# Squares summed on TensorE ahead of two feed-forward stages, and spare matmuls in three places

## The chip, the cores and the metric

The kernel runs on one core of one Trainium2 chip, in one launch. Times are device microseconds of that core. PE is TensorE (matrix products, its results go to PSUM), DVE is VectorE, ACT is ScalarE, POOL is GpSimd and SP is SyncE, which issues most of the transfers. "Granted clock" is the share of full speed at which the profile shows TensorE to run. The metric is the time of one execution. Three runs of the kernel before took 1934.97, 1938.0 and 1938.1 us, median 1938.0.

## The reference

The program computes two layers of a trunk over 512 latent and 256 context tokens of width 1024, all in fp32. Both layers follow the same plan. Layer 0 mixes by differential attention beside a gated DeltaNet, layer 1 by neighbourhood attention on a 64-wide grid; only the latent tokens leave layer 1.

```python
def rms_norm(x, gain):
    xf = x.astype(f32)
    y = xf * lax.rsqrt(jnp.mean(xf * xf, axis=-1, keepdims=True) + EPS)
    return (y * gain.astype(f32)).astype(x.dtype)

def swiglu(h, w_in, w_out):
    gt, up = jnp.split(h @ w_in, 2, axis=-1)
    return (jax.nn.silu(gt) * up) @ w_out
...
        h = rms_norm(x, norm_mix[l]) * (1.0 + sc_m) + sh_m
...
        x = x + g_m * o                      # o: the mixer's output
        hf = rms_norm(x, norm_ffn[l]) * (1.0 + sc_f) + sh_f
        x = x + g_f * swiglu(hf, ffn_w_in[l], ffn_w_out[l])
```

The vectors `sh`, `sc`, `g` come from the conditioning vector by a matrix `ada_w`. The change touches how three of the four `rms_norm` are scheduled, and how two of them sum their squares.

## The kernel before

**Layout.** The activations lie feature-major: `x[k]`, k = 0 to 7, is a tile of 128 features by 768 tokens, the first 256 of them context (`CTX`), the rest latent (`LAT`). Where tokens are treated in pieces, `SEGS` names three segments of 256 tokens: the context and two latent halves. A sum over the features of a token is thus a sum over the eight tiles and over the 128 partitions.

**Products.** Each fp32 product is made of three matmuls of split operands: a high part in the type fp32r and a low part that holds the rest. `mm3` (its matmul is L180) issues high x high, high x low and low x high into one PSUM tile. Weights are split by ACT (a copy, L166) and DVE (a subtraction, L167) in `wsplit`; in the first FFN by `split` (L1519, L1520). Activations are split by the same pair.

**Order.** A framework places the instructions: the program is written as a sequence, and a list scheduler with its own timeline of costs sets the order in which each engine's queue issues them. Each queue is in order afterwards. Buffers come from pools with a tag and a number of buffers; a tile waits for the one that had its buffer before. The PSUM pool `gs` has three tags, A and B with three banks and C with two. So an instruction that is added in one place can move others elsewhere.

**The stages in time.** The first norm is at about 5 to 64 us, the layer-0 mixer up to 680, its output product with the norm ahead of the first FFN (n0f) to about 750, the first FFN and the mixing norm of layer 1 (n1m) to about 1260, the layer-1 mixer to 1550, its output product with the norm ahead of the second FFN (n1f) to 1580, then the second FFN to the end.

**The first norm** (L460 to L560) squares on ACT, adds on DVE (L474), sums over partitions by six matmuls with a vector of ones (L489), and makes the reciprocal root. Then `modulate(j)` makes the scales and shifts of two of the eight tiles: 32 small matmuls (`acc`, L509) from a matrix `aw` that two transfers bring, a copy to a row (DVE, L514), a transpose on TensorE into the PSUM tile `tp` (L516), and the scaling itself, whose results are split into `hhi` (ACT, L534) and `hlo` (DVE, L535). `dense(j, ...)` multiplies these two tiles with the first weights into six PSUM tiles `vp` (L548). The two functions alternate, j = 0 to 3.

**The other norms** are objects of `Norm`. `acc(k, i)` squares tile k of segment i on ACT (L322) and adds the square to `ssq` (L324): on POOL for k below a number, on DVE from it on. `finish(i)` sums over partitions by one matmul for each 128 tokens with the vector of ones as moving operand (L335, PSUM tile `sp`, tag C), takes mean plus epsilon on ACT (`ms`, L337), makes the reciprocal root by a seed and three Newton steps (`rsqrt`, L194 to L206: one operation on DVE, the rest on POOL), and broadcasts it over the partitions with an identity matrix as moving operand (L341, `rb`, tag C). Then eight scalings by DVE (`nt`, L344) read `rb` from PSUM, and `put` shifts and splits them. For the first FFN, `NormS.put` writes them with ACT into `hf` (L383), and `half(0)` and `half(1)` form sums and differences and split them (`split`: ACT L399, DVE L400) into the `v` tiles and others, because this FFN uses the Strassen-Winograd scheme; its products `f` are 128 x 384. The second FFN takes `hhi` and `hlo` (L356, L357) straight, its `f` are 128 x 256 and 128 x 512.

The table `NORMS` gives for each norm the number k from which DVE adds, the engine of the root (G is POOL), and tiles whose split POOL helps with:

```python
NORMS = dict(n0f=(5, 'G', (7,)), n1m=(5, 'G', (7,)), n1f=(4, 'G', ()))
```

**The two places ahead of the FFNs.** For each segment, the loop at L1424 to L1442 makes the eight output tiles of the layer-0 mixer (`o`, six matmuls each for the last two heads, tags A and B), adds them to `x[c]` on DVE (L1435), calls `acc`, and after the eighth `finish`, and from the second segment on `half`. POOL also adds the first weights of the FFN there (`prep`, L1477 to L1480, `ws`), 1.3 us for 512 columns. In layer 1, `oproj` (L1829) does the same for two latent halves (L1866 to L1869), with three matmuls for a tile at the end.

## Time and profile before

| | us |
|---|---|
| median of the three runs | 1938.0 |
| the profiled execution, its own time | 1938.09 |
| its span in the trace | 1936.3 |
| TensorE busy | 1794.5 |
| DVE busy | 1257.4 |
| ACT busy | 805.2 |
| POOL busy | 380.5 |
| TensorE's wait for the reciprocal roots of POOL, all norms | 26.8 |
| mean granted clock | 0.967 |

The slices in the page cut the span into 40 equal parts of 48.4 us; a digit is the busy share of an engine in tenths, and in the row `PEclk` the granted clock. Rows of the table of stretches give the borders in us from the start of the span, the length, the busy time of PE, PEld (loading of weights), DVE, ACT and POOL with their instructions, the granted clock, and the share and rate of the transfers. Rows of a timeline give the start, the duration, the engine, the line, the operation and, in brackets, for how long the engine stood still before it and what ended that. A group's row gives count, busy time, mean duration in ns and the idle time before it.

### The profile page before, as it was taken

Reading aid. Unit: us, or ns where it says so; the run is one execution under the profiler, and the core shown is the slowest. Engines: PE = TensorE matmul, PEld = TensorE weight load, DVE = VectorE, ACT = ScalarE, POOL = GpSimd, SP = SyncE. Lnnn points to the kernel's source line nnn. Section 1 sums busy time; section 2 is a strip of 40 time slices with the busy share of each in tenths; the row PEclk is TensorE's granted clock in tenths of the full one; section 3 lists DMA queues with packets and bytes.
Section 4 is the critical chain, followed back from the end, with each engine's and each line's share of the span. In section 5 each row is a group of like instructions: output and inputs, shape, how many; then the busy total and the mean of one; then the engine's idle time right before and its main releaser. Section 6 shows DMA issues by size and latency. Waiting matters only on the chain.

```text
span 1936.3 us, 30405 instructions
## 1 busy us (share of the span) xinstructions
PE 1794.5 (93%) x11343; PEld 1623.0 (84%) x11343; DVE 1257.4 (65%) x2839; ACT 805.2 (42%) x1773; POOL 380.5 (20%) x436
## 2 busy tenths in 40 slices
PE   4979999788988958999999999899999989999999
PEld 3867889677877857999999999899999778888887
DVE  6566688676767569988877878746666663433333
ACT  3434454446465355232323323455555342222221
POOL 2132214441201052141231322401010020000000
PEclk8989999899999979999999999899999989999999
DMA  7466645656344622424344334212111212323232
GB/s 300 147 192 206 208 128 151 187 158 196 115 122 152 210 83 66 131 98 124 109 138 138 122 122 133 91 45 77 56 62 45 88 45 87 111 78 119 87 105 92
DMA packets 114436, 238.43 MB, mean 123 GB/s; under 512 B 11920, under 2 KB 51088, under 8 KB 113136
## 3 DMA queue, kind: packets, MB, share of 16 engines
q1 hardware_dynamic: 101760, 208.32, 33.8%
q0 software_dynamic: 4064, 14.38, 2.6%
q10 hardware_dynamic: 8464, 13.79, 2.0%
q8 instruction: 90, 1.47, 0.3%
q14 instruction: 58, 0.48, 0.1%
HBM read 203.44 MB, written 32.99 MB: 122 GB/s over the span
## 4 chain that ended last, share of the span: by engine, by line
PE 72%; DVE 6%; DMA 5%; ACT 3%; POOL 2%; issue 2%; SPq 0%; POOLq 0%; ACTq 0%; DVEq 0%
PE f L180 43%; PE d L180 16%; PE o L180 3%; DMA qkd<-ar 1%; PE sc L1779 1%; PE o L1804 1%; PE m L954 1%; PE S L1250 1%; PE t L1278 1%; DMA st<-in_ada_w_dram 1%; PE m L1793 1%; DVE e L1264 0%; PE m L1052 0%; PE m L1750 0%; PE m L1066 0%
## 5 line engine op out<-in xcount | busy, mean ns | idle before, releaser
L166 ACT ACTIVATE whi<-st 128x1024 fp32r<-128x1024 f32 (+6 forms) x191 | 169.6, 889 | 402.7 <-PE f L180 234.3
L167 DVE TENSOR_TENSOR wlo<-st,whi 128x1024 fp32r<-128x1024 f32 (+6 forms) x191 | 195.9, 1027 | 147.7 <-ACT whi L166 145.6
L180 PE MATMUL d<-whi,hhi 128*128 128x256 f32 (+1 forms) x800 | 235.3, 296 | 18.0 <-ACT ar L211 13.6
L180 PE MATMUL d<-wlo,hhi 128*128 128x256 f32 (+1 forms) x800 | 233.2, 292 | 1.3 <-DVE wlo L167 1.3
L180 PE MATMUL d<-whi,hlo 128*128 128x256 f32 (+1 forms) x800 | 232.7, 292 | 0.0
L180 PE MATMUL f<-hlo,whi 128*128 128x512 f32 (+2 forms) x632 | 229.2, 363 | 2.6 <-DVE hlo L400 2.3
L180 PE MATMUL f<-hhi,whi 128*128 128x512 f32 (+2 forms) x632 | 228.5, 363 | 2.6 <-DVE ev L1549 1.3
L180 PE MATMUL f<-hhi,wlo 128*128 128x512 f32 (+2 forms) x632 | 228.2, 362 | 0.3 <-DVE wlo L1520 0.3
L180 PEld LDWEIGHTS d<-whi,hhi 128*128 128x128 f32 x800 | 157.2, 197 | 24.1 <-ACT ar L211 14.9
L180 PEld LDWEIGHTS d<-wlo,hhi 128*128 128x128 f32 x800 | 157.5, 197 | 2.5 <-DVE wlo L167 1.7
L180 PEld LDWEIGHTS d<-whi,hlo 128*128 128x128 f32 x800 | 157.0, 197 | 1.0
L180 PE MATMUL f<-mid,whi 128*128 128x512 f32 (+1 forms) x624 | 151.5, 337 | 0.0
L180 PE MATMUL f<-v,whi 128*128 128x384 f32 x528 | 138.4, 341 | 3.5 <-ACT v L399 2.2
L180 PEld LDWEIGHTS f<-hlo,whi 128*128 128x128 f32 x632 | 119.5, 189 | 16.6 <-DVE hlo L400 2.8
L180 PEld LDWEIGHTS f<-hhi,whi 128*128 128x128 f32 x632 | 119.3, 189 | 16.4 <-ACT hf L383 1.6
L180 PEld LDWEIGHTS f<-hhi,wlo 128*128 128x128 f32 x632 | 119.5, 189 | 13.6 <-DVE wlo L1520 0.5
L180 PEld LDWEIGHTS f<-mid,whi 128*128 128x128 f32 x624 | 106.9, 189 | 12.8
L1477 POOL TENSOR_TENSOR ws<-st 128x512 f32<-128x512 f32 x22 | 33.3, 1511 | 406.0 <-DMA st<-in_wfi_dram 289.9
L180 PE MATMUL d<-hhi,whi 128*128 128x512 f32 (+1 forms) x304 | 107.7, 354 | 2.8 <-ACT cin L211 1.4
L180 PE MATMUL d<-hhi,wlo 128*128 128x512 f32 (+1 forms) x304 | 105.5, 348 | 0.0
L180 PE MATMUL d<-hlo,whi 128*128 128x512 f32 (+1 forms) x304 | 105.4, 347 | 0.0
L180 PE MATMUL f<-mid,wlo 128*128 128x256 f32 (+1 forms) x312 | 102.5, 336 | 0.0
(410 smaller groups left out, 4348.5 us busy)
## 6 DMA issues: line engine op xcount, KB each, us to landing
st<-in_wfi_dram SPq DMA_DIRECT2D x88, 512.0 KB, 3.3
ast<-in_ada_t_dram SPq DMA_DIRECT2D x96, 256.0 KB, 2.9
st<-in_ada_w_dram SPq DMA_DIRECT2D x32, 512.0 KB, 4.0
aw<-in_ada_dram SPq DMA_DIRECT2D x8, 1024.0 KB, 12.5
st<-in_wfo_dram SPq DMA_DIRECT2D x32, 256.0 KB, 2.9
st<-in_w1kv_dram SPq DMA_DIRECT2D x16, 512.0 KB, 3.2
aqT<-qkd SPq DMA_DIRECT2D x48, 128.0 KB, 3.1
st<-in_wfo_dram SPq DMA_DIRECT2D x16, 384.0 KB, 3.0
```

What stands on the lines that cost most here:

```text
L166: S.activation(out=hi, in_=st, func=AF.Copy)
L167: last_lo[:] = [V.tensor_tensor(out=lo, in0=st, in1=hi.bitcast(F32), op=ALU.subtract).ins]
L180: r = T.matmul(out=ps, lhsT=p, rhs=q, start=(c == 0), stop=(c == n - 1))
L954: T.matmul(out=ps[:, i, :], lhsT=lhs[:, c, :], rhs=rhs[:, c, :], start=True, stop=True)
L1250: T.matmul(out=ps[:, o:o + w], lhsT=u.q[:, part, :], rhs=kst[:, m, sl], start=(i == 0), stop=(i == 1))
L1278: T.matmul(out=ov, lhsT=PT[:, i, :], rhs=vt[:, u.kts[i], :], start=(i == 0), stop=(i == u.nk - 1))
L1477: G.tensor_tensor(out=sa[:, 0:512], in0=a21, in1=a22, op=ALU.add)
L1779: T.matmul(out=o, lhsT=lq[:, q], rhs=kv(lk), start=(i == 0), stop=(i == 2))
L1793: T.transpose(out=tp[:, 128 * i:128 * i + 128], in_=E[:, qi, 128 * b:128 * b + 128], identity=ident)
L1804: T.matmul(out=o, lhsT=lv[:, v, :], rhs=p, start=(n == 0 and i == 0), stop=(n == 5 and i == 2))
```

## The change

Three things are changed.

1. For n0f and n1f the squares are no longer added on POOL and DVE. Each square tile goes to TensorE at once: for each 128 tokens one matmul with the square as stationary operand and the vector of ones as moving operand, accumulating over k in one PSUM tile of tag C. n0f has 48 such matmuls where it had 6, n1f 32 where it had 4. The buffers for squares are four instead of two, for n1m too, which otherwise stays as it was.
2. A new function `warm` issues a chain of matmuls of an identity matrix with itself, 128 x 128, into a PSUM tile that nothing reads. It is called with 22 behind the last `o` of n0f, with 16 behind the last `o` of n1f, and with 30 behind the transpose of the first `modulate`, there in the bank of `tp`, which is widened to a whole bank.
3. `mm3`, `oproj` and `modulate` return their last matmul, after which the chain is ordered.

```diff
--- before.py
+++ after.py
@@ -32,7 +32,8 @@
 RS_SEED = -1.8352575e-20
 
 ORDER = "vp0 out1 Ad0 Bd1 vp1 Bd2 Bd3 Ad1 Ad2 G2 G0 Ad3 G1 G3".split()
-NORMS = dict(n0f=(5, 'G', (7,)), n1m=(5, 'G', (7,)), n1f=(4, 'G', ()))
+WARM = (22, 16, 30)
+NORMS = dict(n0f=(None, 'G', (7,)), n1m=(5, 'G', (7,)), n1f=(None, 'G', ()))
 FILL = dict(out1=2, Ad0=1, vp1=2, Ad2=1, G2=3, Ad3=1, G1=3)
 
 CONST_W = {}
@@ -185,6 +186,14 @@
                         tc.add_manual_dep(g.ins, r.ins.name, dep, reason="pace")
                         nops.append(g.ins)
                     c += 1
+            return r.ins
+
+        def warm(pool, tag, pred, n):
+            t = pool.tile([128, 512], F32, name="warm", tag=tag)
+            for _ in range(n):
+                d = T.matmul(out=t[:, 0:128], lhsT=ident, rhs=ident, start=True, stop=True).ins
+                tc.add_manual_dep(d, pred.name, after, reason="warm")
+                pred = d
 
         def rsqrt(pool, v, n, tag="rs", N=None):
             N = N or V
@@ -316,9 +325,21 @@
                 s, sl = self.segs[i]
                 n = sl.stop - sl.start
                 first = self.ssq[i] is None
+                if self.on_v is None:
+                    if first:
+                        self.ssq[i] = self.ps.tile([128, 512], F32, name="sp", tag="C")
+                    sq = self.tile("sq", 256, 4)
+                    S.activation(out=sq, in_=self.x[k][:, sl], func=AF.Square)
+                    m = n // 128
+                    for j in range(m):
+                        self.last = T.matmul(
+                            out=self.ssq[i][:, j:j + 1], lhsT=sq[:, 128 * j:128 * j + 128], rhs=ones,
+                            start=(k == 0 and j == 0), stop=(k == KT - 1 and j == m - 1),
+                        ).ins
+                    return
                 if first:
                     self.ssq[i] = self.tile(f"ssq{i}", n)
-                sq = self.ssq[i] if first else self.tile("sq", 256, 2)
+                sq = self.ssq[i] if first else self.tile("sq", 256, 4)
                 S.activation(out=sq, in_=self.x[k][:, sl], func=AF.Square)
                 if not first:
                     (V if k >= self.on_v else G).tensor_tensor(out=self.ssq[i], in0=self.ssq[i], in1=sq, op=ALU.add)
@@ -330,8 +351,8 @@
                 if self.h is None:
                     self.h = new_h()
                 hi, lo = self.h
-                sp = self.ps.tile([128, 8], F32, name="sp", tag="C")
-                for j in range(m):
+                sp = self.ssq[i] if self.on_v is None else self.ps.tile([128, 8], F32, name="sp", tag="C")
+                for j in range(0 if self.on_v is None else m):
                     T.matmul(out=sp[:, j:j + 1], lhsT=self.ssq[i][:, 128 * j:128 * j + 128], rhs=ones, start=True, stop=True)
                 ms = self.tile("ms", m)
                 S.activation(out=ms, in_=sp[:, 0:m], func=AF.Identity, scale=1.0 / D, bias=epst)
@@ -512,10 +533,10 @@
                         )
                 row = x0p.tile([128, 128], F32, name="row", tag="row", bufs=2)
                 V.tensor_copy(out=row, in_=acc)
-                tp = x0s.tile([128, 128], F32, name="tp", tag="tp")
-                T.transpose(out=tp, in_=row, identity=ident)
+                tp = x0s.tile([128, 512], F32, name="tp", tag="tp")
+                end = T.transpose(out=tp[:, 0:128], in_=row, identity=ident).ins
                 ks = slice(2 * j, 2 * j + 2)
-                tv = tp.rearrange("p (i q u) -> p i q u", i=2, q=2)
+                tv = tp[:, 0:128].rearrange("p (i q u) -> p i q u", i=2, q=2)
                 bv = ada_b[:, 0, 0:16].rearrange("p (i k) -> p i k", i=2)[:, :, ks]
                 for s in range(2):
                     V.tensor_tensor(out=mod[:, s, :, ks], in0=tv[:, :, :, s], in1=bv, op=ALU.add)
@@ -534,6 +555,8 @@
                         S.activation(out=hi[k][:, sl], in_=t, func=AF.Copy)
                         V.tensor_tensor(out=lo[k][:, sl], in0=t, in1=hi[k][:, sl].bitcast(F32), op=ALU.subtract)
 
+                return end
+
             def dense(j, tiles):
                 lab("Bd0")
                 wh, wl = wv[j]
@@ -550,9 +573,11 @@
                                     start=(k == 0 and q == 0), stop=(k == KT - 1 and q == 2),
                                 )
 
-            modulate(0)
+            end = modulate(0)
             for j in range(4):
                 dense(j, (0, 1))
+                if j == 0:
+                    warm(x0s, "tp", end, WARM[2])
                 if j < 3:
                     modulate(j + 1)
                 dense(j, (2,))
@@ -1428,7 +1453,7 @@
             ps = kx.gs.tile([128, sl.stop - sl.start], F32, name="o", tag="AB"[c % 2])
             wh, wl = wo[c // 4]
             o = 256 * (c % 4)
-            mm3(ps, [
+            end = mm3(ps, [
                 (wh[:, o + 128 * i:o + 128 * i + 128], wl[:, o + 128 * i:o + 128 * i + 128], hi2[k][:, sl], lo2[k][:, sl])
                 for i, k in enumerate((6, 7))
             ])
@@ -1436,6 +1461,8 @@
                 out=x[c][:, sl], in0=ps, scalar=scal[0, "g_m", s][:, c:c + 1], in1=x[c][:, sl], op0=ALU.mult, op1=ALU.add,
             )
             kx.n0.acc(c, q)
+        if q == 2:
+            kx.warm(kx.gs, "B", end, WARM[0])
         kx.n0.finish(q)
         if q:
             kx.n0.half(q - 1)
@@ -1828,7 +1855,7 @@
 
         def oproj(c, wh, wl, hs, a0, a1, i):
             ps = gs.tile([128, a1 - a0], F32, name="o", tag="A")
-            mm3(ps, [
+            end = mm3(ps, [
                 (wh[:, k * 128:k * 128 + 128], wl[:, k * 128:k * 128 + 128], mixh[h][:, a0:a1], mixl[h][:, a0:a1])
                 for k, h in enumerate(hs)
             ])
@@ -1837,6 +1864,7 @@
                 out=o, in0=ps, scalar=scal[1, "g_m", 0][:, c:c + 1], in1=o,
                 op0=ALU.mult, op1=ALU.add,
             )
+            return end
 
         TAIL = 1
 
@@ -1864,8 +1892,10 @@
                 for c, (wh, wl) in wt.items():
                     oproj(c, wh, wl, range(7), 256, 512, c)
             for c in range(KT):
-                oproj(c, wb[0][:, 128 * c:128 * c + 128], wb[1][:, 128 * c:128 * c + 128], (7,), 256 * half, 256 * half + 256, c)
+                end = oproj(c, wb[0][:, 128 * c:128 * c + 128], wb[1][:, 128 * c:128 * c + 128], (7,), 256 * half, 256 * half + 256, c)
                 n2.acc(c, half)
+            if half:
+                kx.warm(gs, "B", end, WARM[1])
             n2.finish(half)
     return n2
 
```

The scheduler then puts TensorE's queue in a new order. At the first norm, from the transpose `tp` of modulate(0) on, before:

```order
L516 MATMUL tp<-cst,row 128x128
L509 MATMUL acc<-aw,scT 32x128 x32
L548 MATMUL vp<-hhi_117,whi 128x256 x3
L548 MATMUL vp<-hhi_117,whi 128x512 x3
L516 MATMUL tp<-cst,row 128x128
L548 MATMUL vp<-hlo_125,whi 128x256
```

and with the change (the lines are those of the changed file: L530 is `acc`, L537 `tp`, L571 `vp`, L194 the matmul of `warm`):

```order
L537 MATMUL tp<-cst,row 128x128
L530 MATMUL acc<-aw,scT 32x128 x16
L194 MATMUL warm<-cst 128x128 x19
L571 MATMUL vp<-hhi_117,whi 128x256 x2
L194 MATMUL warm<-cst 128x128 x2
L571 MATMUL vp<-hhi_117,whi 128x512 x2
L194 MATMUL warm<-cst 128x128
L571 MATMUL vp<-hlo_125,whi 128x256
...
L194 MATMUL warm<-cst 128x128 x8
L530 MATMUL acc<-aw,scT 32x128 x16
L571 MATMUL vp<-hhi_117,whi 128x256
```

The second half of the next modulation's `acc`, its transpose, and a part of the `vp` matmuls now stand behind the last eight spare ones.

At n0f, the end of the `o` matmuls and the first `f`, before:

```order
L180 MATMUL o<-hhi_7374,wlo 128x256
L341 MATMUL rb<-cst,rs_y 128x128 x2
L335 MATMUL sp<-cst,ssq_7555 128x1 x2
L341 MATMUL rb<-cst,rs_y 128x128 x2
L335 MATMUL sp<-cst,ssq_7708 128x1 x2
L180 MATMUL f<-v_7684,whi 128x384 x2
```

and with the change, the first `rb` and then the end of the third segment's `o` (L362 is `rb`, L335 the new summing matmul):

```order
L362 MATMUL rb<-cst,rs_y 128x128 x2
L335 MATMUL sp<-cst,sq 128x1 x8
...
L181 MATMUL o<-hhi_7405,wlo 128x256
L194 MATMUL warm<-cst 128x128 x22
L362 MATMUL rb<-cst,rs_y 128x128 x2
L335 MATMUL sp<-cst,sq 128x1 x12
L181 MATMUL f<-v_7729,whi 128x384 x2
L335 MATMUL sp<-cst,sq 128x1 x2
L181 MATMUL f<-v_7730,whi 128x384
```

The first `rb` moved ahead of 23 `o` matmuls, the spare ones stand between the last `o` and the second `rb`, and the third segment's sums stand behind that. Their last pair comes behind twelve `f`, and the third `rb` behind 48; before, fourteen `f` stood ahead of the third `rb`.

At n1f, from the last `o` to the first `f`, before:

```order
L180 MATMUL o<-mh_13168,wlo 128x256
L341 MATMUL rb<-cst,rs_y 128x128 x2
L335 MATMUL sp<-cst,ssq_16904 128x1 x2
L180 MATMUL f<-hhi_16802,whi 128x256 x2
L180 MATMUL f<-hlo_16810,whi 128x256
```

and with the change, from the first `rb` on (between the second and the fourth row stand the last six `o`):

```order
L362 MATMUL rb<-cst,rs_y 128x128 x2
L335 MATMUL sp<-cst,sq 128x1 x6
...
L335 MATMUL sp<-cst,sq 128x1 x2
L194 MATMUL warm<-cst 128x128 x3
L335 MATMUL sp<-cst,sq 128x1 x2
L194 MATMUL warm<-cst 128x128
L335 MATMUL sp<-cst,sq 128x1 x2
L194 MATMUL warm<-cst 128x128 x10
L335 MATMUL sp<-cst,sq 128x1 x4
L194 MATMUL warm<-cst 128x128 x2
L181 MATMUL f<-hhi_16887,whi 128x256
```

Sixteen sums, six `o` and sixteen spare matmuls now stand between the first `rb` and the first `f`. The second `rb` stands behind 48 `f`; before, it stood behind 32.

In POOL's queue the adds are gone. Four weight sums of `prep` stand ahead of the first root of n0f, the first root's operations stand in a row, and two weight sums (L1504, L1505 in the changed file) stand between the last operations of the second; before, two stood inside the first. In ACT's queue the third segment's last five squares stand between the second segment's writes of `hf` and the first splits into `v`, and its mean behind four of these splits. The queues from about 40 to 640 us, those of the layer-0 mixer, are put locally in another order on all engines; those of the layer-1 mixer stand as before.

## The prediction

> **What bounds the kernel now.** I read the page first (busy times, the 40 slices, the chain that ended last), then who ended TensorE's waits, then a table of stretches cut where its granted clock changes, then the rows of those stretches one by one.
>
> ```profile
> span 1936.3 us, 30405 instructions
> PE 1794.5 (93%) x11343; PEld 1623.0 (84%) x11343; DVE 1257.4 (65%) x2839; ACT 805.2 (42%) x1773; POOL 380.5 (20%) x436
> PE   4979999788988958999999999899999989999999
> PEclk8989999899999979999999999899999989999999
> PE 72%; DVE 6%; DMA 5%; ACT 3%; POOL 2%; issue 2%; SPq 0%; POOLq 0%; ACTq 0%; DVEq 0%
> ```
>
> TensorE is busy for 93% of the span and makes 72% of the chain, so whatever is queued on it has a price unless it stands still anyway. The dips of the first two rows are in slices 1 and 2 (the first norm), 8, 11, 14 and 15 (the layer-0 mixer and the norm ahead of its FFN) and 33 (the norm ahead of the second FFN). The waits say what ends these:
>
> ```profile
> PE rb L341 <- POOL rs_y L206: 26.8, 6, 9.4
> PE sp L489 <- DVE ssq L474: 16.4, 1, 16.4
> PE d L180 <- ACT ar L211: 13.6, 4, 6.2
> PE vp L548 <- ACT hhi L534: 4.5, 2, 3.4
> PE f L180 <- DVE hlo L400: 2.3, 2, 2.0
> ```
>
> The largest wait (us in total, times, longest) is that of the broadcast matmuls `rb` for the reciprocal root made on POOL, 26.8 us in six. Taken inside two windows of the same view it is:
>
> ```profile
> PE rb L341 <- POOL rs_y L206: 15.7, 3, 9.4
> PE rb L341 <- POOL rs_y L206: 6.4, 2, 5.7
> ```
>
> 15.7 us ahead of the first FFN (n0f) and 6.4 us ahead of the second (n1f). The 16.4 us before the first norm's sums are the loading of x and are not touched; the `ar` waits are a round trip in the mixer. The stretches (busy time of PE, PEld, DVE, ACT, POOL, then the granted clock):
>
> ```profile
> 37.70:42.60 4.90, 4.85 (x32) 3.98 (x33) 4.76 (x15) 2.44 (x5) 0.00 (x0) 0.50 0.05 18
> 42.60:64.40 21.80, 21.38 (x203) 17.15 (x202) 10.17 (x28) 6.22 (x11) 0.00 (x0) 1.00 0.18 53
> 701.00:710.00 9.00, 0.00 (x0) 0.00 (x0) 2.52 (x6) 3.06 (x8) 8.51 (x18) 0.72 0.00 1
> 721.40:725.00 3.60, 3.54 (x10) 3.03 (x11) 2.69 (x5) 3.57 (x8) 2.96 (x8) 0.50 0.01 2
> 725.00:743.70 18.70, 12.41 (x62) 10.20 (x60) 17.36 (x24) 15.60 (x25) 5.00 (x6) 0.96 0.04 9
> 743.70:749.40 5.70, 5.59 (x17) 5.08 (x18) 5.70 (x8) 0.03 (x1) 0.00 (x0) 0.51 0.71 251
> 766.00:780.00 14.00, 11.75 (x67) 11.11 (x66) 14.00 (x15) 5.84 (x9) 10.54 (x7) 1.00 0.28 92
> 1560.30:1566.00 5.70, 0.04 (x1) 0.00 (x0) 3.40 (x7) 2.46 (x5) 4.86 (x13) 0.62 0.30 93
> 1566.00:1571.80 5.80, 5.06 (x21) 4.68 (x22) 4.50 (x13) 2.74 (x7) 1.95 (x8) 0.50 0.00 0
> ```
>
> In four of them TensorE works at a clock of 0.50 to 0.51, after it stood still: 4.85, 3.54, 5.59 and 5.06 us, 19.0 us in all. And in 725 to 743.7 and 766 to 780 DVE is the full engine (17.36 of 18.7, 14.00 of 14), not TensorE.
>
> **Prices of the parts.** Rows of TensorE's timeline hold two records for one matmul of the program.
>
> ```profile
> 698.19 0.50 PE L335 MATMUL sp<-cst,ssq 128*128 128x1 f32 x4
> 698.55 0.36 PE L180 MATMUL o<-hhi,wlo 128*128 128x256 f32 x1
> 711.08 0.85 PE L335 MATMUL sp<-cst,ssq 128*128 128x1 f32 x4
> 710.07 1.22 PE L341 MATMUL rb<-cst,rs_y 128*128 128x128 f32 x4 [9.37 <-POOL rs_y L206]
> 727.07 0.71 PE L341 MATMUL rb<-cst,rs_y 128*128 128x128 f32 x4 [0.93 <-POOL rs_y L206]
> 727.54 0.77 PE L180 MATMUL f<-v,whi 128*128 128x384 f32 x3
> ```
>
> A summing matmul: two of them take 698.19 to 698.55, so 0.18 us each at full clock; the cold pair 0.85, 0.42 each. A spare matmul has the form of an `rb` matmul (128x128 f32 with the identity as moving operand): two take 727.07 to 727.54, 0.235 each; cold 710.07 to 711.08, 0.50 each. The removed adds and the chain that they sit in:
>
> ```profile
> L324 POOL TENSOR_TENSOR ssq<-ssq,sq 128x256 f32<-128x256 f32 x30 | 24.3, 817 | 82.6 <-ACT sq L322 82.0
> L324 DVE TENSOR_TENSOR ssq<-ssq,sq 128x256 f32<-128x256 f32 x26 | 11.0, 422 | 11.5 <-POOL ssq L324 9.6 <-ACT sq L322 1.1
> 700.35 0.24 POOL L198 TENSOR_SCALAR rs_v<-ms 128x2 f32<-128x2 f32 x1
> 709.80 0.21 POOL L206 TENSOR_TENSOR rs_y<-rs_y,rs_t 128x2 f32<-128x2 f32 x1
> 712.58 0.23 POOL L198 TENSOR_SCALAR rs_v<-ms 128x2 f32<-128x2 f32 x1 [2.57 <-ACT ms L337]
> 717.04 0.20 POOL L206 TENSOR_TENSOR rs_y<-rs_y,rs_t 128x2 f32<-128x2 f32 x1
> ```
>
> A root chain alone takes 712.58 to 717.24, 4.7 us. The first segment's chain, which has adds and weight sums of POOL in between, ran from 700.35 to 710.01.
>
> **First norm.** Thirty spare matmuls. Nineteen fall behind the first half of the next modulation, where TensorE stands still until `hhi` comes (3.4 us of the 4.5 above), and three into the gaps behind; they lie beside DVE and cost nothing. The last eight stand ahead of the remaining `acc` and `vp` matmuls, and from 42.6 on TensorE is the bound (21.38 of 21.80 busy), so they are paid for: 8 x 0.235 = +1.9 us. The gain is that the 4.85 us of matmuls at clock 0.50 may run at full clock sooner: at most half, -2.4. Since TensorE still stands still for hlo between the spare ones and that stretch, I don't take the whole of it, but all but 0.2: **-0.3**, bounds -2.4 (the eight hidden) and +1.9 (no clock gained).
>
> **n0f.** Removed: 3 segments x 3 adds on DVE (9 x 0.42 = 3.8 us) and 3 x 4 on POOL (12 x 0.82 = 9.8). Added: 48 summing matmuls for 6, of which 32 sit among the `o` matmuls or behind them (32 x 0.18 = 5.8 us on an engine that then stands still 9.0 us), and 22 spare (22 x 0.235 = 5.2 us), in front of the second `rb`. The first root chain then runs undisturbed, so the first `rb` moves from 710.07 to about 701 (9.7 us of chain become 4.7, and no add is waited for ahead of it). The `o` matmuls, which ended just ahead of 701, end some 5.4 us later, at about 706; from a sum to its chain it is 1.5 us (711.08 to 712.58), the chain 4.7, and two weight sums now stand inside it, some 1.3 each (an add of half the elements has 0.82 in the mean, so this is an estimate): the second `rb` at about 714.8 for 717.29. For the third the last squares stand, in the new order, behind ACT's scalings and splits of the second. I estimate eight scalings, four splits and five squares at 0.4 to 0.9 us each, some 8 to 9 us, then 1.5 to the chain and 4.7 of chain: its `rb`, which came at 727.07, comes between 729 and 731; I take 729.5, +2.4, near the early end, since the squares and scalings are the shorter ones. What decides is DVE, which is full from 725 on: it has 3.8 us less to do and gets its third segment 2.4 us later: **-1.4**. Bounds: -5.6 (all of the 3.8, and half of the 3.54 cold us at 721.4 saved by the spare matmuls), +1.0 (the third segment late by twice that, with DVE standing still for it).
>
> **n1f.** Rows of the stretch before:
>
> ```profile
> 1558.22 0.22 POOL L198 TENSOR_SCALAR rs_v<-ms 128x2 f32<-128x2 f32 x1 [3.45 <-ACT ms L337]
> 1566.04 1.22 PE L341 MATMUL rb<-cst,rs_y 128*128 128x128 f32 x4 [5.70 <-POOL rs_y L206]
> 1568.37 0.80 PE L180 MATMUL f<-hhi,whi 128*128 128x256 f32 x2 [0.47 <-ACT hhi L356]
> 1571.92 0.28 PE L180 MATMUL f<-hhi,whi 128*128 128x256 f32 x1
> 1572.04 0.28 PE L180 MATMUL f<-hlo,whi 128*128 128x256 f32 x1
> 1575.00 0.71 PE L341 MATMUL rb<-cst,rs_y 128*128 128x128 f32 x4 [0.66 <-POOL rs_y L206]
> 1577.46 0.63 PE L180 MATMUL f<-hhi,whi 128*128 128x256 f32 x3
> ```
>
> The first chain starts at 1558.22; without the adds in it, it takes 4.7 us and `rb` comes at 1562.9, 3.1 earlier. But behind it in TensorE's queue, ahead of the first `f`, now stand the pair of `rb` (0.47), 16 summing (16 x 0.18 = 2.9), 6 `o` (6 x 0.12 = 0.7, by the step from 1571.92 to 1572.04) and 16 spare matmuls (16 x 0.235 = 3.8), 7.9 us: the first `f` starts at 1570.8 for 1568.37, although its input is there at 1562.9 + 2.33 = 1565.2. From there 48 `f` at 0.12 (5.8 us, at full clock, where before the first ones were cold) end at 1576.5, and only then does the second `rb` come; before it came at 1575.00 with some 16 `f` behind it as cover for the scaling. Now nothing covers that: 2.33 us by the first pair, less the 0.54 by which a warm pair is shorter than a cold one, so the second half's first `f` is at 1578.3 where it was at 1577.46: **+0.9**. Bounds: -0.5 (the later wait of 0.6 for hhi goes too), +2.7 (the clock has fallen before the first `rb`, and the next 3.6 us of work, as from 721.4 to 725, take double, +1.8).
>
> **The rest.** Four buffers for squares instead of two, the wider `tp` tile and the second mixer: its queues stand in the same order as before, so 0. The layer-0 mixer's queues are locally put in another order from 40 to 640 us, loads of weights and the round trip `ar` among them; nothing says with which sign. It is bounded by a part of the 13.6 us of `ar` waits, one third either way, 4.5; I take 0.
>
> **Sum.** -0.3 - 1.4 + 0.9 + 0 = -0.8. The profiled execution took 1938.1 us (1936.3 of span and 1.8 around it); the median of the runs, 1938.0, is the same. So 1938.1 - 0.8 = **1937.3**. What a measurement of this kernel can tell from no change is about 0.2%, 3.9 us, so this is no measurable change.
>
> **The rivals.** *The cold stretches go* (faster). The clock is at 0.62 in the standstill at 1560.3 and 0.50 in the work behind it, and 0.72 then 0.50 at n0f; each time it fell while TensorE stood still. If the spare matmuls hold it up at all three places, half of the 19.0 us goes: -9.5, 1928.6. For it: the rows of the clock. Against it: the stretch at 743.7 stands behind a wait for hlo on DVE that the spare matmuls do not reach, and in n1f the first standstill is ahead of them. [...]
>
> *The queue on TensorE* (slower). Summing and spare matmuls stand in order ahead of work that is ready, most of all at n1f. It decides there from when the first `rb` comes: if that stays at 1566.04, because its chain on POOL still waits, the 7.9 us of queue begin 3.1 later and the clock has fallen (+1.8): +0.9 becomes +5.8. With the same at the first norm, where the eight spare ones are paid in full without gain (+1.9), and n0f at -1.4: 1938.1 + 5.8 + 1.9 - 1.4 = 1944.4. From `rb` at about 1564 on it is a measurable loss. For it: TensorE makes 72% of the chain, and the 48 `f` no longer cover the second `rb`. Against it: no add is left in POOL's chain.
>
> *The mixer's order* decides, though the change does not aim there: 1937.3 with 4.5 either way, 1932.8 or 1941.8 and beyond. For it: a wait of 6.2 us for `ar` hangs on when transfers are issued; against it: the same instructions wait for the same transfers.
>
> **Chances.** The three places cancel: 0.38. Cold stretches go: 0.30. The queue: 0.20. The mixer's order: 0.12, half to each side. So faster by over 0.2% has 0.36, within it 0.38, slower 0.26. The range goes from just above the fast rival's 1928.6, whose whole gain I do not expect, to just under the slow one's 1944.4: 1929 to 1944. The forecast's own range, from the bounds of its terms taken in quadrature (4.9 down, 3.7 up, the mixer's left out), is 1932.4 to 1941.
>
> **What would show it.** The waits for `rb` should shrink from 22.1 us at the two norms to some 5, and the clock at 1566 to 1572 be full. First norm: the granted clock between 37.7 and 42.6, and the end of the 21.8 us stretch. n0f: the first `rb` near 701, the third near 729.5, DVE still full up to 750. n1f: the first `rb` near 1562.9, the first `f` near 1570.8, a gap of about 1.8 us behind the second `rb`. (All are counted from the same point of the span, less what came earlier or later before it.) The forecast is wrong if the stretch 743.7 to 749.4 comes out at full clock, if the third segment's squares are not late, if `rb` at n1f is later than 1564, or if the mixer's end moves by over 4 us against the first norm's.

## The result, and the profile after

The changed kernel takes 1961.9 us (median of 4 runs, 1959.8 to 1970.0) for 1938.1 before: a ratio of 1.0132, with a 95% interval of 1.0107 to 1.0157. It is 24 us slower, outside the range of the forecast and on the other side of no change from where the sum lay. Single executions of one kernel scatter by several us (the kernel before was between 1930 and 1949 in all its runs here), so ratios below stand with their intervals.

The page of the changed kernel, the lines that answer to those of before (its profiled execution took 1959.83 us):

```profile
span 1957.9 us, 30914 instructions
PE 1825.0 (93%) x11619; PEld 1655.1 (85%) x11619; DVE 1260.7 (64%) x2822; ACT 807.0 (41%) x1773; POOL 358.3 (18%) x418
PE   5978899798987988999999999899999999999999
PEclk8989999989998998999999999999999989999999
PE 63%; DVE 3%; DMA 1%; POOL 1%; issue 1%; ACT 1%; POOLq 0%; DVEq 0%; ACTq 0%; SPq 0%
```

TensorE is busy 30.5 us longer and POOL 22 us shorter, as the change has it. The mean granted clock even rose, from 0.967 to 0.971. Who ended TensorE's waits now:

```profile
PE sp L510 <- DVE ssq L495: 16.4, 1, 16.4
PE d L181 <- ACT ar L220: 9.2, 2, 5.9
PE adacc L251 <- DMA st<-in_ada_w_dram: 8.2, 3, 5.3
PE rb L362 <- POOL rs_y L215: 8.0, 4, 4.5
PE S L1275 <- DMA akT<-qkd: 6.6, 2, 5.2
PE f L181 <- ACT hhi L420: 6.0, 1, 6.0
```

(`adacc` are products of the streamed matrix `ada_w` inside the mixer, `ar` is the round trip named before, `S` are attention scores.) The wait for `rb`, which was the largest of the change's own places, went from 26.8 to 8.0 us over all norms, and from 22.1 to 3.1 at the two norms of the forecast, which said some 5. That is not where the time is. To find it, both traces are cut at the same events: the first `d` matmul of the layer-0 mixer, the first `o` of its output, the first FFN product of `mid` (what the first weights of the FFN give), and the last attention product of layer 1. The table of stretches of the kernel before, then of the changed one (borders and length in us, busy PE, PEld, DVE, ACT, POOL, granted clock):

```profile
0.00:64.30 64.30, 39.13 (x392) 31.48 (x393) 39.77 (x83) 21.84 (x34) 12.80 (x10) 0.89 0.63 237
64.30:681.40 617.10, 547.14 (x3903) 484.64 (x3901) 427.64 (x1194) 305.91 (x751) 144.24 (x153) 0.95 0.56 171
681.40:796.30 114.90, 89.20 (x505) 84.99 (x506) 95.02 (x160) 55.98 (x102) 46.30 (x70) 0.87 0.22 73
796.30:1548.40 752.10, 744.19 (x4829) 709.21 (x4828) 540.12 (x1191) 312.05 (x731) 163.56 (x169) 0.99 0.31 99
1548.40:1936.30 387.90, 374.86 (x1719) 312.69 (x1718) 154.89 (x214) 109.39 (x157) 13.56 (x34) 0.99 0.29 91
```

```profile
0.00:68.70 68.70, 46.06 (x453) 38.53 (x453) 39.08 (x79) 21.49 (x33) 12.79 (x10) 0.93 0.58 222
68.70:702.20 633.50, 550.29 (x3903) 486.32 (x3903) 439.57 (x1198) 309.86 (x752) 142.23 (x153) 0.95 0.54 167
702.20:812.90 110.70, 98.97 (x633) 97.53 (x634) 89.49 (x151) 56.11 (x102) 33.41 (x58) 0.92 0.22 74
812.90:1564.60 751.70, 743.55 (x4829) 708.39 (x4828) 541.19 (x1191) 310.37 (x731) 163.69 (x169) 1.00 0.31 99
1564.60:1957.90 393.30, 386.09 (x1807) 324.32 (x1806) 151.41 (x206) 109.16 (x157) 6.16 (x28) 0.99 0.28 90
```

The lengths differ by +4.4 (first norm), **+16.4** (layer-0 mixer), -4.2 (n0f), -0.4, and +5.4 (n1f): +21.6 in all. The mixer's 3903 records of matmuls are the same work in both; 3.2 us of its 16.4 are busy time, 13.2 us are TensorE standing still. The change works in three places; the largest difference came from a fourth, which it does not touch in the program text and which the sum had at 0.

### The profile page after: what moved, and what is told of

Same layout as the page of the kernel before. It is cut to its first block, busy times and chain, and to the rows that moved or that the text cites. A ratio compares the mean times of both kernels' runs of the same rounds, so it can differ in the third digit from the quotient of the medians.

```text
span 1957.9 us, 30914 instructions
## 1 busy us (share of the span) xinstructions
PE 1825.0 (93%) x11619; PEld 1655.1 (85%) x11619; DVE 1260.7 (64%) x2822; ACT 807.0 (41%) x1773; POOL 358.3 (18%) x418
## 4 chain that ended last, share of the span: by engine, by line
PE 63%; DVE 3%; DMA 1%; POOL 1%; issue 1%; ACT 1%; POOLq 0%; DVEq 0%; ACTq 0%; SPq 0%
PE f L181 43%; PE d L181 11%; PE o L181 3%; PE sc L1806 1%; PE o L1831 1%; PE sp L335 1%; PE m L1820 1%; PE m L1777 0%; DVE nt L365 0%; DVE hlo L421 0%; PE t L1303 0%; DVE hlo L1371 0%; DMA x1d<-xc 0%; PE rb L362 0%; PE warm L194 0%
## 5 line engine op out<-in xcount | busy, mean ns | idle before, releaser
L1504 POOL TENSOR_TENSOR ws<-st 128x512 f32<-128x512 f32 x22 | 32.4, 1474 | 411.9 <-DMA st<-in_wfi_dram 286.9
```

The lines of the kernel that those rows point to most:

```text
L1504: G.tensor_tensor(out=sa[:, 0:512], in0=a21, in1=a22, op=ALU.add)
```

## Whose are the 20 us ahead of n0f

My theory after the result: the thirty spare matmuls at the first norm make the list scheduler put the mixer in another order, and that order is worse. The rivals: the spare matmuls cost by themselves, by what they delay; or the sums and the four buffers for squares have a part in it. Four kernels, each cut out of the changed one (`warm` returns at once for a number of 0; where `NORMS` is put back, squares have two buffers again, so that nothing of the change is left but the spare matmuls and the wider `tp` tile).

```diff
 e1_first30
-WARM = (22, 16, 30)
-NORMS = dict(n0f=(None, 'G', (7,)), n1m=(5, 'G', (7,)), n1f=(None, 'G', ()))
+WARM = (0, 0, 30)
+NORMS = dict(n0f=(5, 'G', (7,)), n1m=(5, 'G', (7,)), n1f=(4, 'G', ()))
 e2_no_first
-WARM = (22, 16, 30)
+WARM = (22, 16, 0)
 e3_first6, e4_first10: as e1_first30, with
+WARM = (0, 0, 6)
+WARM = (0, 0, 10)
```

> Only the thirty spare matmuls of the first norm are added to the kernel before; the sums and the other spare matmuls are left as before. Its queues in the layer-0 mixer stand exactly as in the changed kernel. If the loss ahead of n0f (20.7 us, of it 4.3 up to the first d of the mixer) comes from this part alone, the time is 1938 + 20 to 21 = about 1958 to 1959, the first f of the first FFN some 20 us later than before, and nothing changes behind it. If it comes from the sums or buffers of squares, the time is near 1938 + 4 = 1942.

> The change without the first norm's thirty spare matmuls; sums and spare matmuls ahead of both FFNs stay. The queues up to the first FFN's norm stand as in the kernel before. If the parts add up: -4.1 at n0f and +5.4 at n1f, so 1938 + 1.3 = about 1939. If the loss in the mixer comes from the four buffers for squares or the sums, it stays near 1960. My own prediction's terms would give 1938 - 1.4 + 0.9 = 1937.5.

> Only six spare matmuls at the first norm, in the standstill ahead of hhi; the order of all other instructions is that of the kernel before, but for one pair at the first norm. If spare matmuls cost only through the new order, 1938 within 1 us. If a spare matmul itself sets off the loss (a bank, a wait, the clock), some of the 20 us is there: by their number 6/30, 4 us.

> Ten spare matmuls at the first norm, all in the same standstill (10 x 0.235 = 2.35 us of 3.4 to 4.2), nothing else changed; but from here on the mixer's queues stand in another order, a third one, neither that of before nor that with thirty. If the order is what costs, the time moves by many us, either way, though four more hidden matmuls cannot cost it: outside 1934 to 1942. If the number of spare matmuls is what costs, 10/30 of 20, or rather none since they are hidden: 1938 to 1945.

| kernel | median, us | ratio to before, 95% interval |
|---|---|---|
| e1_first30 | 1958.6 | 1.0111 (1.0083 to 1.0139) |
| e2_no_first | 1944.1 | 1.0027 (1.0011 to 1.0043) |
| e3_first6 | 1940.0 | 1.0003 (0.9987 to 1.0020) |
| e4_first10 | 1957.8 | 1.0114 (1.0088 to 1.0139) |

The first norm's part alone costs 1.11%, all the rest 0.27%; that is 1.38%, for the 1.32% of the change, well within the intervals. (The rest was expected to cost about 1 us, by the lengths in one trace, and costs 5: a miss, taken up at n1f below.) Between six and ten spare matmuls lies the whole loss, although all ten lie in a standstill of TensorE. What changes between six and ten is the order: with six the mixer's queues stand as before, with ten they don't, in the traces of the two kernels. The mixer's stretch, from first `d` to first `o`, in the run with six and in the run with ten:

```profile
64.80:684.80 620.00, 546.35 (x3904) 483.79 (x3902) 430.27 (x1194) 305.57 (x751) 145.43 (x153) 0.95 0.56 170
```

```profile
64.00:700.20 636.20, 554.27 (x3904) 488.01 (x3902) 421.48 (x1197) 305.33 (x747) 140.79 (x153) 0.94 0.53 165
```

The run with ten enters the mixer at 64.2, not later than before (64.3), and takes 636.2 us for it, 16.2 more than the run with six: 7.9 us of that are busy time for the same matmuls (the granted clock is 0.94 for 0.95), and 8.3 are standstill. So the loss is not passed on from the first norm; it arises behind it. The slow orders so far have spare matmuls in common, though. Two further counts, and then three kernels with no spare matmul:

```diff
 e11_first22, e12_first14: as e1_first30, with
+WARM = (0, 0, 22)
+WARM = (0, 0, 14)
 e13_swap_scale: the kernel before, with (in modulate)
-                    for s, sl in ((1, CTX), (0, LAT)):
+                    for s, sl in ((0, LAT), (1, CTX)):
 e14_swap_dense: the kernel before, with (in dense)
-                    for s, sl in ((0, CTX), (1, LAT)):
+                    for s, sl in ((1, LAT), (0, CTX)):
 e15_rb_dve: the kernel before, with (in the first norm)
-                    S.activation(out=rb[:, sl], in_=bp, func=AF.Copy)
+                    V.tensor_copy(out=rb[:, sl], in_=bp)
```

> Twenty-two spare matmuls at the first norm alone: without the last eight, so all of them hidden; the mixer's queues stand in yet another order. If new orders cost about the same wherever they come from (two of two so far: +19 and +20), 1950 to 1960. If they are spread about the old one, some of them are as fast or faster: anything from 1925 to 1960, and this says how wide.

> Fourteen spare matmuls at the first norm alone, all in the standstill; the mixer's order is close to that with thirty in its first part (same loads), another one later. If the order sets the time: as with thirty less the 3 to 4 us that the eight unhidden ones and what stands behind them cost, about 1955. If orders scatter: anything from 1925 to 1960.

> The kernel before with no instruction added: in the first norm the scalings are written for the latent tokens ahead of the context's, instead of behind. The scheduler then puts the mixer in another order. If any other order of the mixer costs some 12 to 20 us and the old one is a rare good one: 1950 to 1960. If the loss comes with spare matmuls (what they delay, what they do to the clock or to loads), and orders by themselves scatter about the old one: 1930 to 1946.

> The kernel before with no instruction added: the first dense products are written for the latent tokens first. Again another order of the mixer. As above: 1950 to 1960 if the old order is a rare good one, 1930 to 1946 if the loss belongs to the spare matmuls.

> The kernel before, with the two copies of the first norm's broadcast root from PSUM made by DVE in place of ACT: no spare matmul, some 0.2 us of difference at the first norm by itself, and a further order of the mixer. As above: 1950 to 1960 if the old order is a rare good one, 1930 to 1946 if the loss belongs to the spare matmuls.

| kernel | median, us | ratio to before, 95% interval | first `d` to first `o` in its trace, us |
|---|---|---|---|
| before | 1938.1 | | 617.1 |
| e3_first6 (order of before) | 1940.0 | 1.0003 | 619.9 |
| e15_rb_dve | 1948.0 | 1.0036 (1.0014 to 1.0059) | 628.9 |
| e13_swap_scale | 1955.4 | 1.0076 (1.0047 to 1.0105) | 630.3 |
| e14_swap_dense | 1957.0 | 1.0077 (1.0053 to 1.0101) | 636.1 |
| e11_first22 | 1957.5 | 1.0095 (1.0066 to 1.0123) | 630.9 |
| e1_first30 | 1958.6 | 1.0111 (1.0083 to 1.0139) | 637.1 |
| e4_first10 | 1957.8 | 1.0114 (1.0088 to 1.0139) | 636.2 |
| e12_first14 | 1963.8 | 1.0128 (1.0095 to 1.0161) | 629.8 |

Two kernels with the same matmuls and vector operations as before and one `for` tuple swapped in each lose some 15 us. (Their new order costs ACT two more loads of function tables, 1.28 us each in the trace of before; the run with ten has two fewer than before and is as slow.) All seven new orders are slower than the old one (the changed kernel has the order of e1_first30), the mixer by 12 to 20 us against the one trace of before; over the nine kernels with the old order that stretch is 614.0 to 619.9 us. So spare matmuls aren't needed for the loss, and that orders scatter evenly about the old one does not fit: the old order is the good one among eight. The seven are not independent draws, however: TensorE's queues of e1_first30 and e12_first14 are nearly the same, and those of e11_first22, e13_swap_scale and e14_swap_dense resemble each other.

With more than ten spare matmuls the first norm adds 3 to 4.6 us of its own (their first `d` comes at 67.3 to 68.9). And the border at the first `o` cuts a part of the loss off: from there to the first product of `mid` it is 118.4 to 120.5 us in the runs with 10, 14 and 22 spare matmuls and in the two with swaps, for 114.8 in the kernel before and 113.3 in the run with six, which have the same instructions there.

Two of the expectations were misses: e12_first14 was to take 1955, at most 1960, and took 1963.8; e15_rb_dve lies between the two ranges that it was to decide between, and the interval of its ratio lies above 1 all the same.

Where in the mixer the time goes is spread out. TensorE's waits in the run with ten, the longest ones, inside the mixer:

```profile
PE d L181 <- ACT ar L222: 11.2, 3, 6.2
PE t L1300 <- ACT PT L222: 7.4, 6, 2.7
PE p L823 <- ACT p L855: 7.2, 3, 5.5
PE S L1277 <- DMA akT<-qkd: 4.8, 1, 4.8
...
PE t L1305 <- ACT PT L222: 4.1, 2, 3.5
PE m L987 <- DVE oacc L1067: 3.9, 1, 3.9
```

and in the run with swapped scalings:

```profile
PE d L180 <- ACT ar L211: 18.7, 5, 6.8
PE adacc L242 <- DMA st<-in_ada_w_dram: 8.9, 4, 5.5
PE S L1250 <- DMA akT<-qkd: 5.6, 2, 4.0
PE t L1273 <- ACT PT L211: 5.1, 4, 2.7
```

The wait of the attention scores `S` for `akT`, keys that come back from memory, takes 3.6 to 7.4 us in the traces of all seven new orders (6.6 in the changed kernel), and 0 to 1.9 us in those of the nine kernels with the old order, the one before among them. That is the one common part found, and at most some 60% of the mixer's loss, in most orders less than half; the rest differs from order to order (the run with ten waits less for `ar` than the kernel before, the run with swapped scalings more). Which exchange of instructions makes these waits is open: no run puts back a part of the old order.

## n1f: the clock falls while TensorE is busy

Without the first norm's part 5 us are left (e2_no_first), and its trace puts 3.4 of them at n1f. The queue of spare matmuls was my suspect. The trace of the changed kernel showed something else: three stretches of 3.4 and 6.8 us of n1f's output stage. (In its trace and in that of before, all changes of the granted clock lie a multiple of 3.41 us apart.)

```profile
1565.80:1569.20 3.40, 3.06 (x21) 2.68 (x22) 2.58 (x6) 1.69 (x5) 0.00 (x0) 1.00 0.00 0
1569.20:1572.60 3.40, 3.40 (x32) 3.40 (x31) 1.50 (x4) 1.35 (x4) 0.00 (x0) 0.99 0.00 0
1572.60:1579.40 6.80, 6.80 (x33) 6.80 (x34) 0.92 (x3) 0.68 (x2) 1.34 (x7) 0.50 0.00 0
```

In the second TensorE is busy for all of the 3.40 us, and then the clock is half for 6.8 us. What runs there are mostly three `o` matmuls and then a pair of summing matmuls, in turn. My theory, a guess from these rows: the clock falls because the summing matmuls move one column each, though they keep the engine occupied (0.18 us each). The rival: the spare matmuls and the queue. The second kernel gives every summing matmul 128 equal columns (the mean on ACT then reads every 128th column, in a line that is not shown):

```diff
 e5_n1f_sums
-WARM = (22, 16, 30)
-NORMS = dict(n0f=(None, 'G', (7,)), n1m=(5, 'G', (7,)), n1f=(None, 'G', ()))
+WARM = (0, 0, 0)
+NORMS = dict(n0f=(5, 'G', (7,)), n1m=(5, 'G', (7,)), n1f=(None, 'G', ()))
 e6_n1f_wide: the same, and
-    out=self.ssq[i][:, j:j + 1], lhsT=sq[:, 128 * j:128 * j + 128], rhs=ones,
+    out=self.ssq[i][:, 128 * j:128 * j + 128], lhsT=sq[:, 128 * j:128 * j + 128], rhs=ones.to_broadcast([128, 128]),
```

> Only n1f's squares go to TensorE (32 summing matmuls for 4 and the adds removed); no spare matmul anywhere, n0f as before. In the run without the first norm's spare matmuls n1f cost 3.4 us, and the granted clock fell at 1558.1 without a standstill, in the midst of the summing matmuls. If the 16 spare matmuls (3.8 us of queue ahead of ready f) are what costs there, n1f is now at -0.4: 1938.3. If the sums cost, because the clock falls during them, +2 or more stays: 1940.7 or more, and the trace shows half clock ahead of the first rb, which then is not earlier than 1566.

> As the run with n1f's sums alone, but each summing matmul moves 128 equal columns of ones instead of one (some 0.235 us for 0.18), so that TensorE's array is at work for longer in it. If the clock falls in the sums because matmuls of one column hardly count as work, it now stays at 1.00 until the standstill ahead of the first rb, the o matmuls of the second half take 0.12 and not 0.21 each, and the first rb comes 2 to 3 us earlier than in that run, for 32 x 0.055 = 1.8 us more of queue: 1 us faster than it or equal. If the fall has another cause (the phase of the clock's windows alone), the clock falls here too and the time is 1.8 us longer than in that run.

The sums alone, with no spare matmul anywhere, take 1943.8 us, 1.0030 (1.0017 to 1.0043). With wide sums it is 1937.4, 0.9998 (0.9982 to 1.0014), 6 us less where at most 1 was expected. The stretches of the two, first one column:

```profile
1552.20:1555.60 3.40, 3.40 (x33) 3.40 (x31) 2.45 (x6) 2.47 (x7) 0.00 (x0) 1.00 0.02 5
1555.60:1559.00 3.40, 3.40 (x19) 3.40 (x20) 0.16 (x1) 0.42 (x1) 0.00 (x0) 0.57 0.00 0
1559.00:1562.40 3.40, 3.40 (x18) 3.40 (x17) 0.17 (x1) 0.26 (x1) 0.46 (x3) 0.50 0.00 0
```

then 128 columns:

```profile
1549.40:1552.80 3.40, 3.40 (x32) 3.40 (x31) 2.06 (x5) 2.19 (x6) 0.00 (x0) 1.00 0.03 5
1552.80:1556.20 3.40, 3.40 (x32) 3.40 (x32) 0.17 (x1) 0.41 (x2) 0.18 (x1) 1.00 0.00 0
1556.20:1559.60 3.40, 3.40 (x28) 3.27 (x26) 2.98 (x8) 1.45 (x4) 2.41 (x13) 1.00 0.01 2
```

The same busy time, another clock. And the wide sums are no dearer in the queue (rows of one pair of each and the next `o`):

```profile
1552.68 0.50 PE L337 MATMUL sp<-cst,sq 128*128 128x1 f32 x4
1553.04 0.36 PE L181 MATMUL o<-mh,whi 128*128 128x256 f32 x1
```

```profile
1549.32 0.60 PE L337 MATMUL sp<-cst,sq 128*128 128x128 f32 x4
1549.68 0.37 PE L181 MATMUL o<-mh,whi 128*128 128x256 f32 x1
```

0.36 us for two in both, by the starts; that TensorE's array is at work for longer with 128 columns was my estimate, and these rows do not show it. Measured from the last attention product, the first `rb` of n1f comes after 17.7 us before, 18.7 with sums of one column and 14.7 with wide ones; the program's last matmul ends after 384.1, 389.1 and 382.0 us. The theory fits as far as it speaks of columns: in all three kernels with one-column sums at n1f that were profiled (the change, e2_no_first, e5_n1f_sums) the clock fell to half 7.4 to 8.0 us behind the last attention product, with TensorE busy; with wide sums (three kernels) or with adds on POOL it did not fall there. How rare that is shows when the 17 traces are cut into the steps of 3.41 us at whose borders the granted clock changes: over 8000 steps at full clock have TensorE busy for more than 2.5 us, and only three of them are followed by half clock, these three. More than 200 have it busy for less than 1.5 us, and half clock follows every one; a step need not be idle throughout. These three falls last 6.8 or 10.2 us, two and three such steps, and idle time does not explain them: in the step ahead of each TensorE was busy for 3.40 of 3.40 us. By what the clock is set, no run shows.

## n0f, and both places together

```diff
 e7_n0f_only
-WARM = (22, 16, 30)
-NORMS = dict(n0f=(None, 'G', (7,)), n1m=(5, 'G', (7,)), n1f=(None, 'G', ()))
+WARM = (22, 0, 0)
+NORMS = dict(n0f=(None, 'G', (7,)), n1m=(5, 'G', (7,)), n1f=(4, 'G', ()))
 e8_n0f_sums: the same with
+WARM = (0, 0, 0)
 e9_both_wide: e6_n1f_wide, with n0f=(None, 'G', (7,)) too
 e10_both_wide_spare: e9_both_wide with
+WARM = (22, 16, 0)
```

> Only n0f: its sums on TensorE and its 22 spare matmuls; the first norm and n1f as before. In the run without the first norm's spare matmuls n0f cost about 2.6 us by its trace: the first rb came 9.5 us earlier, the second 2.5 earlier, the third 3.7 later. If that is n0f's own, this run is at 1938.7 + 2.6 = 1941.3. My term of -1.4 would give 1937.3.

> As the run with n0f alone, without its 22 spare matmuls. They stood in the standstill ahead of the second rb (707 to 712), which comes at 714.8 by the chain on POOL. If spare matmuls there neither cost nor gain: the same time as with them. If they keep the clock up for what follows: this run is slower by up to half of the cold f, 2 us, and the clock falls by 711. If they hold up something, it is faster by up to 2 us, with a second rb ahead of 714.

> n0f and n1f with sums on TensorE, every summing matmul moving 128 columns, no spare matmul anywhere; the mixer's order is that of the kernel before. If one-column sums let the clock fall at n0f too, the clock now holds through the o stage and the 12 sums behind the second rb, and n0f gains 1 to 3 us; with the 2.1 us that n1f gained by its trace in the run with wide sums (its end 382.0 us behind the last attention product for 384.1 before) the time is 1939 - 3 to -5 = 1934 to 1936. If the clock at n0f is set by the standstills alone, n0f stays at 0 or +1 (48 x 0.055 us more): 1937 to 1938.

> As the run with wide sums at both places, with the 22 and 16 spare matmuls of the change ahead of the FFNs. If spare matmuls help by keeping the clock up: 1 to 2 us faster than that run. If at n1f they stand ahead of ready work: 4 to 12 of the 16 lie in the wait for the first rb, four behind it: equal or up to 1 us slower.

n0f alone takes 1938.6 us, 1.0003 (0.9992 to 1.0014); without its spare matmuls 1937.3, 0.9996 (0.9981 to 1.0012). Neither its sums nor its 22 spare matmuls move the time measurably. From the first `o` to the first product of `mid` it is 114.8 us before, 116.0 and 115.1 in these two; the changed kernel's own 110.8 is not seen again in a kernel with the old mixer's order, and why is open (there the `o` stage began at full clock, in these three with 3.4 us of half clock from 681 to 685 on). The expected 1941.3 was a miss: the 2.6 us that I read at n0f in one trace did not come back. The spare matmuls don't hold the clock for what follows, as the trace of e2_no_first shows:

```profile
707.47 5.07 PE L196 MATMUL warm<-cst 128*128 128x128 f32 x44
715.01 1.09 PE L364 MATMUL rb<-cst,rs_y 128*128 128x128 f32 x4 [2.47 <-POOL rs_y L217]
```

```profile
715.00:725.20 10.20, 10.19 (x44) 10.19 (x45) 6.50 (x13) 7.93 (x17) 1.49 (x3) 0.51 0.00 1
```

They end at 712.5, 2.5 us ahead of the second `rb`, and from 715.0 on 10.2 us of sums and first `f` run at half clock. The sums have a part in that too: sixteen of them take 6.7 us at half clock, TensorE is busy throughout, and the clock does not come back before they are over. In the trace of e10_both_wide_spare below, with the same 22 spare matmuls and wide sums, the half clock at this place lasts 3.4 us.

Wide sums at both places: 1938.2 us, 0.9998 (0.9981 to 1.0015); with the 22 and 16 spare matmuls 1937.7, 0.9991 (0.9973 to 1.0009). The first expectation, 1934 to 1936, was a miss; the second, 1937 to 1938 if standstills alone set the clock at n0f, fits: it falls all the same, with standstills inside (10.2 us each from 713.3 and 737.2). With n1f's sixteen spare matmuls, four of them behind the first `rb`, the time from the last attention product to the last matmul is 386.6 us for 383.9 without, in one trace each: where the clock holds anyway, they look like a queue alone. Several of these versions beat the changed kernel; none is measurably faster than the kernel before.

## Why the prediction was wrong

**The step that failed** is "the rest": the layer-0 mixer's new order was seen and taken at 0, "bounded by a part of the 13.6 us of `ar` waits, one third either way, 4.5". It cost 16.4 us in the profiled execution, and each of the seven new orders costs 12 to 20 in the mixer alone. That the mixer's end would move by over 4 us against the first norm's was one of the signs of being wrong that the prediction named. Two things were wrong in it. The bound was taken from one wait, while the new orders lose by many (13.2 us of standstill, none of it more `ar`: that wait is 9.2 us now for 13.6). And the sign was taken as open, while the old order is the best of the eight that ran; whether it was chosen or is luck is not on record. The rival on the mixer's order had the right place, 0.12 of chance and a quarter of the size.

**First norm:** -0.3 forecast, +4.4 in the trace, outside the bounds of -2.4 to +1.9. The last eight spare matmuls take their 1.9 us where TensorE bounds; the gain of clock, which I took nearly whole, did not come:

```profile
33.20:43.40 10.20, 6.63 (x22) 5.46 (x22) 8.07 (x12) 3.27 (x5) 4.46 (x3) 0.50 0.49 191
```

```profile
44.04 1.95 PE L194 MATMUL warm<-cst 128*128 128x128 f32 x16
45.91 1.08 PE L530 MATMUL acc<-aw,scT 128*32 128x128 f32 x32
46.92 0.39 PE L571 MATMUL vp<-hhi,whi 128*128 128x256 f32 x1
```

The clock fell at 33.2, behind 3.3 us in which TensorE was busy for 1.2, and stayed half until 43.4, over the first 5.4 us of the work that begins at 38.0 (4.85 us before); between the spare matmuls and that work TensorE stood still for 3.6 us. On top of 1.87 us for the eight, 1.01 us of `acc` and two cold `vp` were moved out of the standstill into the stretch that TensorE bounds. The moved `acc` was named ahead of the prediction, and not counted. These parts do not explain the 4.4 us by themselves: e11_first22, which lacks the last eight, reaches its first `d` just as late, at 68.8, though its work behind `hlo` begins only 1.1 us later than the changed kernel's. What the new order of `acc` and `vp` costs there no run separates.

**n0f:** -1.4, against +0.6 by time with an interval of -1.6 to +2.7: not to be told from it. The walk through the three `rb` was right: `rb` at 700.7, 715.0 and 730.9 in the kernel without the first norm's part, for 701, 714.8 and 729 to 731.

**n1f:** +0.9 forecast, 5 us measured (+5.8 for the sums alone, 3.3 to 8.3). The queue was sized well: 8.3 us from the first `rb` to the first `f` (1581.54 to 1589.85) for 7.9. What failed is the price of a sum: 0.18 us each and nothing else, where their real price is the clock that they let fall, for the `o` matmuls as well. The first `rb` came 17.0 us behind the last attention product and not 3.1 earlier than the old 17.7. The slow rival had the size, +5.8, by luck: it has a late `rb` and a fallen clock too, but from POOL's chain and from a standstill, with the spare matmuls as its queue, and the loss is as large without any of them. (The term's lower bound, -0.5, does not come out of its own figures either: 0.9 less 0.6 is +0.3. And the slices in which the prediction sees the dips are counted partly from 0 and partly from 1. Neither moves the forecast, and the lower end of its own range only by 0.2 us.)

**The fast rival** fell: the clock's share rose only from 0.967 to 0.971, and the work behind the spare matmuls was cold at the first norm and at n0f.

## What to carry to other kernels

Where a list scheduler sets the order, a few instructions more, even hidden ones, can redraw the order of a whole stage behind them, and of an order that was good the redraw is a loss: compare the queues first, price a reordered stretch by what other orders of it cost, and put such an edit in only where the queues behind it stay. At n1f, with one-column matmuls among its work, TensorE was busy for 3.40 of 3.40 us and its clock then fell to 0.50; with 128 columns, in the same time (0.36 us for two), it stayed at 1.00. Spare matmuls gained no time in any kernel here; where 2.5 to 3.6 us of standstill lay between the last of them and the work that they were meant for, that work began at half clock.

## What the runs showed of the hardware that I had not expected

The granted clock went to half with TensorE busy in the whole 3.40 us ahead of it, when 1.8 to 1.9 us of these were pairs of one-column fp32 matmuls between 128x256 ones (by their starts in the timeline); with 128 columns each, at the same 0.18 us, it stayed at 1.00. In the `o` stages of n0f, where the pairs make up to 1.7 us of a 3.4 us step, it stayed at 1.00 too (702.2 to 736 in the changed kernel), and so it did behind one step of e5_n1f_sums with 2.0 us of them (1566.4 to 1569.8). So the share of such pairs alone does not settle it, and no run varies that share by itself.
